# Attention of a hybrid transformer block: stacked query operands, a pinned last score group, and key tiles in reverse

## The chip, the cores and the metric

The kernel runs on one core of a Trainium2 chip. TensorE multiplies matrices (in the profile: PE, with PEld for the loading of the stationary operand), VectorE is DVE, ScalarE is ACT, GpSimd is POOL, and SyncE (SP) issues most transfers from memory. [...] The metric is the device time of one launch in microseconds: a median of repeated runs, beside one execution that was profiled.

## The reference

Two layers, each of a mixer and a gated feed-forward part, on 512 tokens of width 1024. The mixer projects the tokens and splits them over three kinds of heads: eight dilated attention heads of width 64, four retention heads and four gated linear attention (GLA) heads. The attention heads are what the change touches:

```python
qa = apply_rope(split_heads(qa, N_HEADS_A), cos_a, sin_a)
ka = apply_rope(split_heads(ka, N_HEADS_A), cos_a, sin_a)
va = split_heads(va, N_HEADS_A)
ya = merge_heads(head_norm(dilated_attention(qa, ka, va)))
...
scores = jnp.einsum('bhrnqd,bhrnkd->bhrnqk', qb, kk).astype(jnp.float32) * (d ** -0.5)
...
p = jnp.exp(scores - m[..., None])
l = p.sum(-1)
o = jnp.einsum('bhrnqk,bhrnkd->bhrnqd', p, vv) / l[..., None]
```

The three dilated branches are weighted by their denominators and summed. With 512 tokens this equals one causal softmax in which a key counts as often as branches see it; the kernel holds these counts in a constant table (`mult`).

The mixer's output goes through `w_out`, a residual and a layer norm; then a feed-forward part follows with a three-tap causal convolution and a gate, again with a residual and a norm.

## The kernel before, in words

**Precision.** The large products run with float32r operands, each value split into a high part and the rounded rest, the low part. `mm3` (lines 211 to 214) adds three products: high by high, high by low, low by high. A weight tile comes by DMA into `raw`, ScalarE casts it to `whi` (line 198), and VectorE subtracts to get `wlo` (line 199). The tokens stand in `xth` and `xtl`, transposed. In the profile's names the moving operand comes first: `acc<-xth,whi` streams tokens against stationary weights (the query and key projections of the heads), `acc<-whi,xth` streams weights against stationary tokens (v, gates, output).

**Attention, by pairs of heads.** Head pair p holds heads 2p and 2p+1, on the partition rows 0 to 63 and 64 to 127. `project_heads(g)` (lines 588 to 611) makes two pairs: for query and key it runs 8 x 3 matmuls into an `acc` bank, turns the result by the rotary tables (ScalarE copies at line 604, VectorE at 605 to 607), casts it to a high part `qk` (line 608) and subtracts for the low part (line 610).

`scores` (lines 613 to 645) goes through the query tiles of 128 tokens in three groups: tile 3, tile 2, tiles 0 and 1 together. For every tile and both heads it issues three products with 64 rows (line 629): high query by high key, high query by low key, low query by high key. Each group takes two `bank`s, one for each head, out of four; VectorE reads a bank with the mask and takes the row minimum (line 638), ScalarE takes the exponential (line 641), VectorE multiplies by the counts and sums (line 642).

`weighted` (lines 647 to 682) transposes the probabilities on TensorE (line 286), ScalarE copies them out (line 671), and products with v (line 659) are summed over the key tiles in one bank, in the groups key tile 0, key tiles 1 and 3, key tile 2. Then follow a copy, transposes back, and `finish` with the norm of the head; `finish_rows` transposes the finished rows for the output projection.

**What sets the order.** The kernel is written as a program without an order of its own between engines: a planner takes, on every engine, the instruction with the lowest priority number among those it holds to be ready by its own estimate of the times, and gives out buffers as it goes. `at(n)` sets the number from which the next instructions count. What results is a fixed list for every engine, and each engine works its list in order. `tc.issue_after(x)` forces the instructions traced in its block to stand behind instruction x on x's engine. In a layer the numbers are: heads 0 and 1 at 5000, scores of pair 0 at 6000 and pair 1 at 6400, v at 7000, heads 2 and 3 at 8000, scores of pair 2 at 9000 and pair 3 at 9400, gates at 9200, output projection at 20000.

**Buffers.** `x4` has three tiles of 128 x 4 x 512, for the query and key operands, for v, and for the norms' gains `gb` (loaded by GpSimd's queue, line 740); `bank` has four PSUM banks for scores, transposes and attention output; `page` has nine tiles of 128 x 512.

Of the kernel before, what the change touches and what calls it, by code (L numbers as in the profile page):

```python
# [17 lines left out]
P = 128  # L18
# [131 lines left out]
def hymba(ctx: ExitStack, tc: tile.TileContext, x, xt, wpk, prm, wal, lnv, cst, out):  # L150
# [59 lines left out]

    def mm3(ps, ah, al, bh, bl, first, last):
        nc.tensor.matmul(ps, ah, bh, start=first, stop=False)  # L212
        nc.tensor.matmul(ps, ah, bl, start=False, stop=False)  # L213
        nc.tensor.matmul(ps, al, bh, start=False, stop=last)  # L214
# [199 lines left out]
    for l in range(DEPTH):  # L414
# [173 lines left out]
        def project_heads(g):  # L588


            qk = x4("qk", F32R)
            low = [None] * 4
            for u in range(2):
                kt = chunk(l, f"heads{2 * g + u}")
                for qk_ in range(2):
                    b = 2 * qk_ + u
                    ps = acc()
                    ms = slice(qk_ * P, (qk_ + 1) * P)
                    for k in range(KD):
                        h_, l_ = kt[k]  # L600
                        mm3(ps, h_[:, ms], l_[:, ms], xth[:, k, :], xtl[:, k, :], k == 0, k == KD - 1)
                    turned, a = page("rope"), page("rope")
                    for r in range(4):
                        A.copy(turned[32 * r:32 * r + 32, :], ps[32 * (r ^ 1):32 * (r ^ 1) + 32, :])
                    V.tensor_mul(a, ps, C("ropea_c"))
                    V.tensor_mul(turned, turned, C("ropea_s"))
                    V.tensor_add(a, a, turned)
                    A.copy(qk[:, b, :], a)
                    low[b] = page("yrg", 512, F32R)
                    V.tensor_sub(low[b], a, qk[:, b, :].bitcast(F32))  # L610
            return qk, low

        def scores(qk, low, u, l3):


            probs = [[None] * NT, [None] * NT]
            nmx = small(8, "s_at")
            for group in ((3,), (2,), (0, 1)):
                scs = [bank(), bank()]
                prs, o = [page(), page()], 0  # L620
                for i in group:
                    n, m = (i + 1) * P, max(256, (i + 1) * P)
                    ts = slice(i * P, (i + 1) * P)
                    for step in range(3):
                        for hh in range(2):
                            hs = slice(hh * 64, hh * 64 + 64)
                            q_ = (low[u][hs, ts] if step == 2 else qk[hs, u, ts])
                            k_ = (low[2 + u][hs, 0:m] if step == 1 else qk[hs, 2 + u, 0:m])
                            mmul(scs[hh][:, o:o + m], q_, k_, start=step == 0, stop=step == 2)  # L629
                    for hh in range(2):  # L630
                        probs[hh][i] = (scs[hh][:, o:o + n], prs[hh][:, o:o + n])
                    o += m
                for hh in range(2):
                    for i in group:
# [3 lines left out]
                        V.tensor_tensor_reduce(out=p_, in0=s_, in1=C("neg")[:, m0:], op0=ALU.add, op1=ALU.min,  # L638
                                               scale=-0.125, scalar=3e38, accum_out=mx)
                        with tc.issue_after(tables.ins):  # L640
                            A.activation(out=p_, in_=p_, func=AF.Exp, scale=-1.0, bias=mx)
                        V.tensor_tensor_reduce(out=p_, in0=p_, in1=C("mult")[:, m0:], op0=ALU.mult, op1=ALU.add,
                                               scale=1.0, scalar=0.0, accum_out=l3[:, i, hh:hh + 1])
                        probs[hh][i] = p_
            return probs

        def weighted(pr, c0):


            groups = ((0,), (1, 3), (2,))  # L650
# [48 lines left out]
        for g in range(2):  # L699
            at(base + 5000 + 3000 * g)  # L700
            qk, low = project_heads(g)
            if g == 0:
                at(base + 7000)
                vv = x4("v")
                kt = chunk(l, "v")
                for t in range(NT):
                    centred(project(kt, t, 512), vv[:, t, :], "s_v")
            for u in range(2):
                at(base + 6000 + 3000 * g + 400 * u)
                p2 = 2 * g + u  # L710
# [7 lines left out]

        at(base + 9200)
        kt = chunk(l, "gates")  # L720
        for t in range(NT):
            ps = project(kt, t, 512)
            g = page("rope")
            with tc.issue_after(tables.ins):
                A.activation(out=g, in_=ps, func=AF.Tanh, scale=0.5)
            V.scalar_tensor_tensor(out=g, in0=g, scalar=1.0, in1=ps, op0=ALU.add, op1=ALU.mult)
            V.tensor_mul(ynat[t], ynat[t], g)
# [134 lines left out]
```

## Time and profile before

| | us |
|---|---|
| median of 3 runs | 1248.39 (1246.88 to 1251.35) |
| profiled execution, whole time | 1247.36 |
| its span | 1245.6 |
| PE busy | 1227.3 |
| DVE busy | 785.2 |
| ACT busy | 490.6 |
| granted TensorE clock | 0.997 of full |

The span is the time from the first to the last instruction of the profiled execution. A timeline row reads: start, duration, engine, line, operation, result and operands, shape of the stationary tile and of the moving one, count; in brackets the idle time of the engine before it and what ended that. Matmuls overlap in the pipeline, so the cost of one is the distance to the next one's start and not its duration. A row with x2 holds two instructions merged. A row of the waits reads: who waited for whom, total us, times, longest us. In the rows of groups the numbers after the bar are busy us, mean ns of one, and idle us of the engine before them.

In the first layer the span's stages on TensorE around the change are: projection of heads 0 and 1 (until 100.6 us, mixed with the retention and GLA products), scores of pair 0, v (102.1 to 131.2), heads 2 and 3 (131.2 to 166.6, with the scores of pair 1 from 135.5), scores of pair 2, gates (168.0 to 199), scores of pair 3 (from 199.4), output projection (from 204.4).

### The profile page before, as it was taken

To read this page: it belongs to the slowest core of one execution; us is meant where nothing else is said; L and a number is where in the kernel's file an instruction comes from. 1 tells how busy PE (TensorE), PEld (TensorE's weight loads), DVE (VectorE), ACT (ScalarE), POOL (GpSimd) and SP (SyncE) were. 2 spreads that over 40 slices of the span, in tenths; PEclk is the share of its full clock that TensorE was granted. 3 is DMA by queue.
4 is the path that set the end of the run, shared out by engine and by line. 5 is a ranking of instruction groups with operands and counts; after the bars stand their busy time and mean duration, and the time that the engine had idled before them with its cause. 6 is when DMAs were issued, how large, how long until landed. Compare 5 with 4: busy or idle time off the path is not lost.

```text
span 1245.6 us, 15209 instructions
## 1 busy us (share of the span) xinstructions
PE 1227.3 (99%) x5956; PEld 999.1 (80%) x5956; DVE 785.2 (63%) x1451; ACT 490.6 (39%) x689; POOL 17.0 (1%) x26
## 2 busy tenths in 40 slices
PE   9999999999999999999999999999999999999997
PEld 7877677898888888888887776778988888888885
DVE  6685776777663356664767857677766633566636
ACT  4434565145442134442153446552444421444410
POOL 0000000000000000000000000000000000000000
PEclk9999999999999999999999999999999999999998
DMA  8411313223332333232142113131333323333221
GB/s 293 131 64 34 118 51 99 72 74 130 100 89 91 93 111 91 87 100 77 62 132 88 34 43 128 34 119 51 102 117 89 100 76 98 114 102 102 93 77 68
DMA packets 33399, 116.27 MB, mean 93 GB/s; under 512 B 3728, under 2 KB 4144, under 8 KB 33200
## 3 DMA queue, kind: packets, MB, share of 16 engines
q1 hardware_dynamic: 32176, 111.11, 28.5%
q0 software_dynamic: 1152, 4.19, 0.9%
q8 instruction: 47, 0.77, 0.2%
q14 instruction: 24, 0.20, 0.1%
HBM read 113.20 MB, written 2.10 MB: 93 GB/s over the span
## 4 chain that ended last, share of the span: by engine, by line
PE 91%; DVE 4%; DMA 2%; ACT 2%; issue 0%; SPq 0%; DVEq 0%; ACTq 0%
PE acc L214 25%; PE acc L213 25%; PE acc L212 25%; PE bk L286 3%; PE side L213 2%; PE side L212 2%; PE side L214 2%; DMA raw<-in_wpk 2%; PE bk L659 2%; DVE wlo L199 1%; ACT whi L198 1%; DVE pg L638 1%; PE bk L565 1%; PE bk L545 1%; PE bk L561 1%; PE bk L629 1%
## 5 line engine op out<-in xcount | busy, mean ns | idle before, releaser
L199 DVE TENSOR_TENSOR wlo<-raw,whi 128x1024 fp32r<-128x1024 f32 (+2 forms) x201 | 240.1, 1195 | 218.7 <-ACT whi L198 217.4
L213 PE MATMUL acc<-xtl,whi 128*128 128x512 f32 (+1 forms) x896 | 341.8, 382 | 0.0
L212 PE MATMUL acc<-xth,whi 128*128 128x512 f32 (+1 forms) x896 | 341.7, 382 | 0.0
L214 PE MATMUL acc<-xth,wlo 128*128 128x512 f32 (+1 forms) x896 | 339.6, 379 | 0.0
L198 ACT CAST whi<-raw 128x1024 fp32r<-128x1024 f32 (+2 forms) x201 | 206.2, 1026 | 321.0 <-PE side L214 139.8
L214 PEld LDWEIGHTS acc<-xth,wlo 128*128 128x128 f32 x896 | 168.6, 188 | 35.2 <-issue 4.0
L213 PEld LDWEIGHTS acc<-xtl,whi 128*128 128x128 f32 x896 | 168.6, 188 | 34.2 <-issue 3.5
L212 PEld LDWEIGHTS acc<-xth,whi 128*128 128x128 f32 x896 | 168.4, 188 | 31.8 <-issue 1.5
L212 PE MATMUL acc<-whi,xth 128*128 128x512 f32 (+1 forms) x256 | 94.4, 369 | 0.6 <-ACT whi L198 0.6
L213 PE MATMUL acc<-wlo,xth 128*128 128x512 f32 (+1 forms) x256 | 94.3, 368 | 0.7 <-DVE wlo L199 0.7
L214 PE MATMUL acc<-whi,xtl 128*128 128x512 f32 (+1 forms) x256 | 94.7, 370 | 0.0
L212 PE MATMUL acc<-whi,yt 128*128 128x512 f32 x238 | 93.2, 393 | 0.0
L213 PE MATMUL acc<-wlo,yt 128*128 128x512 f32 x238 | 92.3, 389 | 0.0
L214 PE MATMUL acc<-whi,yt 128*128 128x512 f32 x238 | 92.3, 389 | 0.0
L765 DVE SCALAR_TENSOR_TENSOR pg<-acc,prm,pg 128x511 f32<-128x511 f32 x86 | 64.2, 747 | 31.7 <-ACT pg L764 31.7
L764 ACT ACTIVATE pg<-acc,prm 128x512 f32<-128x512 f32 x86 | 66.8, 777 | 26.3 <-PE acc L214 26.3
L766 DVE SCALAR_TENSOR_TENSOR pg<-acc,prm,pg 128x510 f32<-128x510 f32 x86 | 64.4, 749 | 3.0
L388 DVE SCALAR_TENSOR_TENSOR x<-x,acc 128x512 f32<-128x512 f32 x38 | 26.1, 686 | 59.7 <-PE acc L214 59.7
L213 PEld LDWEIGHTS acc<-wlo,xth 128*128 128x128 f32 x256 | 48.1, 188 | 9.2 <-DVE wlo L199 1.1
L212 PEld LDWEIGHTS acc<-whi,xth 128*128 128x128 f32 x256 | 48.3, 189 | 8.8 <-issue 1.0
L214 PEld LDWEIGHTS acc<-whi,xtl 128*128 128x128 f32 x256 | 48.1, 188 | 8.7 <-issue 1.2
L212 PE MATMUL acc<-whi,yrg 128*128 128x512 f32 x138 | 54.5, 395 | 0.0
(176 smaller groups left out, 1541.4 us busy)
## 6 DMA issues: line engine op xcount, KB each, us to landing
raw<-in_wpk SPq DMA_DIRECT2D x188, 512.0 KB, 3.6
gb<-in_lnv POOLq DMA_DIRECT2D x8, 512.0 KB, 4.7
x<-in_x SPq DMA_DIRECT2D x4, 512.0 KB, 6.3
raw<-in_wpk SPq DMA_DIRECT2D x8, 256.0 KB, 2.8
out<-x SPq DMA_DIRECT2D x8, 256.0 KB, 2.0
raw<-in_wpk SPq DMA_DIRECT2D x4, 408.0 KB, 3.3
xraw<-in_xt SPq DMA_DIRECT2D x3, 512.0 KB, 7.4
cst<-in_cst SPq DMA_DIRECT2D x1, 1478.0 KB, 9.3
```

The source lines that it names most:

```text
L198: nc.scalar.copy(hi, raw)
L199: lo_engine.tensor_sub(lo, raw, hi.bitcast(F32))
L212: nc.tensor.matmul(ps, ah, bh, start=first, stop=False)
L213: nc.tensor.matmul(ps, ah, bl, start=False, stop=False)
L214: nc.tensor.matmul(ps, al, bh, start=False, stop=last)
L286: nc.tensor.transpose(dst, src, ident)
L388: V.scalar_tensor_tensor(out=xr, in0=xr, scalar=scale, in1=ps, op0=ALU.mult, op1=ALU.add)
L545: mmul(sc, kT[:, ts], qbd, start=True, stop=True)
L659: mmul(oT[hh * 64:hh * 64 + 64, j * P:], vv[:, j, c0 + hh * 64:c0 + hh * 64 + 64], pts[hh][:, o:o + n], start=j == 0, stop=js == groups[-1])
L764: A.activation(out=u, in_=ps, func=AF.Identity, scale=w(2), bias=w(3))
L765: V.scalar_tensor_tensor(out=u[:, 1:], in0=ps[:, :S - 1], scalar=w(1), in1=u[:, 1:], op0=ALU.mult, op1=ALU.add)
L766: V.scalar_tensor_tensor(out=u[:, 2:], in0=ps[:, :S - 2], scalar=w(0), in1=u[:, 2:], op0=ALU.mult, op1=ALU.add)
```

## The change

- `project_heads` makes one pair at a time and writes four operands into one `x4` tile. For head A of the pair, `qA` holds the high query in rows 0 to 63 and the low query in rows 64 to 127, `kA` the high key in both halves. `qB` and `kB` are the same for head B with the halves exchanged. `kl` holds the low keys of both heads.
- `scores` forms a score tile from one product with 128 rows (high and low query by high key) and one with 64 rows (high query by low key). Query tiles 3 and 2 are issued as one block, all 128-row products first and then the 64-row ones; tiles 0 and 1 follow in a block of the same form.
- The block of tiles 0 and 1 is forced behind a given product on TensorE: for pair 0 behind the fourth `mm3` of v, for pair 1 behind the eleventh of heads 2 and 3, for pair 2 behind the fourth of the gates; pair 3 has none. For this the gates' code stands ahead of the scores of pairs 2 and 3 in the source; priorities are as before.
- `weighted` goes through the keys as tiles 2 and 3, then tile 1, then tile 0.

```diff
+    made = []
+
     def mm3(ps, ah, al, bh, bl, first, last):
         nc.tensor.matmul(ps, ah, bh, start=first, stop=False)
         nc.tensor.matmul(ps, ah, bl, start=False, stop=False)
-        nc.tensor.matmul(ps, al, bh, start=False, stop=last)
+        made.append(nc.tensor.matmul(ps, al, bh, start=False, stop=last).ins)
...
-        def project_heads(g):
-            qk = x4("qk", F32R)
-            low = [None] * 4
-            for u in range(2):
-                kt = chunk(l, f"heads{2 * g + u}")
...
-                    A.copy(qk[:, b, :], a)
-                    low[b] = page("yrg", 512, F32R)
-                    V.tensor_sub(low[b], a, qk[:, b, :].bitcast(F32))
-            return qk, low
+        def project_heads(p):
+            four = x4("qk", F32R)
+            qA, qB, kA, kB = (four[:, i, :] for i in range(4))
+            kl = page("yrg", 512, F32R)
+            up, dn = slice(0, 64), slice(64, 128)
+            kt = chunk(l, f"heads{p}")
...
+                if b == 0:
+                    A.copy(qA[up], a[up])
+                    A.copy(qB[dn], a[dn])
+                    V.tensor_sub(qA[dn], a[up], qA[up].bitcast(F32))
+                    V.tensor_sub(qB[up], a[dn], qB[dn].bitcast(F32))
+                else:
+                    A.copy(kA[up], a[up])
+                    A.copy(kB[dn], a[dn])
+                    A.copy(kA[dn], a[up])
+                    A.copy(kB[up], a[dn])
+                    V.tensor_sub(kl[up], a[up], kA[up].bitcast(F32))
+                    V.tensor_sub(kl[dn], a[dn], kB[dn].bitcast(F32))
+            return qA, qB, kA, kB, kl
 
-        def scores(qk, low, u, l3):
+        def scores(parts, l3, behind):
+            qA, qB, kA, kB, kl = parts
...
-            for group in ((3,), (2,), (0, 1)):
...
-                    for step in range(3):
-                        for hh in range(2):
-                            hs = slice(hh * 64, hh * 64 + 64)
-                            q_ = (low[u][hs, ts] if step == 2 else qk[hs, u, ts])
-                            k_ = (low[2 + u][hs, 0:m] if step == 1 else qk[hs, 2 + u, 0:m])
-                            mmul(scs[hh][:, o:o + m], q_, k_, start=step == 0, stop=step == 2)
+            def products(banks, places, half):
+                for i, (g_, o) in places.items():
+                    m = max(256, (i + 1) * P)
+                    ts = slice(i * P, (i + 1) * P)
+                    for hh in range(2):
+                        hs = slice(hh * 64, hh * 64 + 64) if half else slice(0, P)
+                        mmul(banks[g_][hh][:, o:o + m], (qA, qB)[hh][hs, ts], (kl, kl)[hh][hs, :m] if half else (kA, kB)[hh][:, :m],
+                             start=not half and o == 0, stop=half and i > 0)
+
+            for groups in (((3,), (2,)), ((0, 1),)):
...
+                with tc.issue_after(behind) if behind and len(groups) == 1 else nullcontext():
+                    for half in (False, True):
+                        products(banks, places, half)
...
-            groups = ((0,), (1, 3), (2,))
+            groups = ((2, 3), (1,), (0,))
...
-                             pts[hh][:, o:o + n], start=j == 0, stop=js == groups[-1])
+                             pts[hh][:, o:o + n], start=j == 2, stop=j == 0, skip_group_check=True)
...
-        for g in range(2):
-            at(base + 5000 + 3000 * g)
-            qk, low = project_heads(g)
-            if g == 0:
+        marks = {}
+        for two in range(2):
+            if two == 0:
+                at(base + 5000)
+                parts = [project_heads(p) for p in range(2)]
                 at(base + 7000)
                 vv = x4("v")
+                marks["v"] = len(made)
...
+                at(base + 8000)
+                marks["heads"] = len(made)
+                parts += [project_heads(p) for p in range(2, 4)]
+            else:
+                at(base + 9200)
+                marks["gates"] = len(made)
+                kt = chunk(l, "gates")
...
-                pr = scores(qk, low, u, l3)
+                name, n = (("v", 3), ("heads", 10), ("gates", 3), (None, 0))[p2]
+                pr = scores(parts[p2], l3, made[marks[name] + n] if name else None)
                 finish_rows()
                 o = weighted(pr, p2 * P)
                 finish(o, ll, p2)
```

More of the change, by code (lines that the diff above doesn't have):

```diff
@@ L1 @@
 import math
-from contextlib import ExitStack
+from contextlib import ExitStack, nullcontext
 import numpy as np
@@ L585, in hymba @@
                 nc.sync.dma_start(out=xres[t], in_=x[t * P:(t + 1) * P, :])
-        def project_heads(g):
-            qk = x4("qk", F32R)
-            low = [None] * 4
-            for u in range(2):
-                kt = chunk(l, f"heads{2 * g + u}")
[L595 to L608, printed above, removed]
-                    low[b] = page("yrg", 512, F32R)
-                    V.tensor_sub(low[b], a, qk[:, b, :].bitcast(F32))
-            return qk, low
@@ L613, in scores @@
-        def scores(qk, low, u, l3):
+        def project_heads(p):
[4 more added lines that the diff above has]
+            kt = chunk(l, f"heads{p}")
+            for b in range(2):
+                ps = acc()
+                ms = slice(b * P, (b + 1) * P)
+                for k in range(KD):
+                    h_, l_ = kt[k]
+                    mm3(ps, h_[:, ms], l_[:, ms], xth[:, k, :], xtl[:, k, :], k == 0, k == KD - 1)
+                turned, a = page("rope"), page("rope")
+                for r in range(4):
+                    A.copy(turned[32 * r:32 * r + 32, :], ps[32 * (r ^ 1):32 * (r ^ 1) + 32, :])
+                V.tensor_mul(a, ps, C("ropea_c"))
+                V.tensor_mul(turned, turned, C("ropea_s"))
+                V.tensor_add(a, a, turned)
+                if b == 0:
[11 more added lines that the diff above has]
+            return qA, qB, kA, kB, kl
@@ L707, in hymba @@
                     centred(project(kt, t, 512), vv[:, t, :], "s_v")
+                at(base + 8000)
[5 more added lines that the diff above has]
+                kt = chunk(l, "gates")
+                for t in range(NT):
+                    ps = project(kt, t, 512)
+                    g = page("rope")
+                    with tc.issue_after(tables.ins):
+                        A.activation(out=g, in_=ps, func=AF.Tanh, scale=0.5)
+                    V.scalar_tensor_tensor(out=g, in0=g, scalar=1.0, in1=ps, op0=ALU.add, op1=ALU.mult)
+                    V.tensor_mul(ynat[t], ynat[t], g)
             for u in range(2):
-                at(base + 6000 + 3000 * g + 400 * u)
-                p2 = 2 * g + u
+                at(base + 6000 + 3000 * two + 400 * u)
+                p2 = 2 * two + u
                 ll = small(8, "s_at")
                 l3 = ll.rearrange("p (i h) -> p i h", h=2)
-                pr = scores(qk, low, u, l3)
+                name, n = (("v", 3), ("heads", 10), ("gates", 3), (None, 0))[p2]
+                pr = scores(parts[p2], l3, made[marks[name] + n] if name else None)
                 finish_rows()
@@ L719, in hymba @@
         at(base + 9200)
[L720 to L727, printed above, removed]
         for k in range(4):
```

18 lines of the change are left out of this document (10 added, 8 removed).

## The prediction

> **What bounds the kernel now.** I read the page first: which engine fills the span, and what the chain that ended last is made of.
>
> ```profile
> span 1245.6 us, 15209 instructions
> PE 1227.3 (99%) x5956; PEld 999.1 (80%) x5956; DVE 785.2 (63%) x1451; ACT 490.6 (39%) x689; POOL 17.0 (1%) x26
> PE 91%; DVE 4%; DMA 2%; ACT 2%; issue 0%; SPq 0%; DVEq 0%; ACTq 0%
> ```
>
> TensorE is busy for 1227.3 of 1245.6 us and holds 91% of the chain. So time is won only where TensorE's instructions become fewer or cheaper, or where it stands still. Next I asked who TensorE waits for, over the whole span.
>
> ```profile
> PE bk L629 <- DVE s_at L638: 4.4, 6, 0.9
> ```
>
> The largest wait is in attention: score products (L629) standing behind the VectorE pass that reads an earlier score bank (L638), three times in each layer. Being "busy" also hides slow stretches, since the ends of matmuls are modelled, so the third view is TensorE's timeline, where I read the distance from one start to the next. Here is head pair 0 of the first layer, with the VectorE row it waits for.
>
> ```profile
> 100.12 0.39 PE L213 MATMUL acc<-xtl,whi 128*128 128x512 f32 x1
> 100.35 0.39 PE L214 MATMUL acc<-xth,wlo 128*128 128x512 f32 x1
> 100.67 0.50 PE L629 MATMUL bk<-qk 64*128 64x512 f32 x2
> 101.00 0.40 PE L629 MATMUL bk<-yrg,qk 64*128 64x512 f32 x2
> 101.24 0.40 PE L629 MATMUL bk<-qk,yrg 64*128 64x512 f32 x2
> 101.47 0.34 PE L629 MATMUL bk<-qk 64*128 64x384 f32 x2
> 101.63 1.23 DVE L199 TENSOR_TENSOR wlo<-raw,whi 128x1024 fp32r<-128x1024 f32 x1
> 101.65 0.34 PE L629 MATMUL bk<-yrg,qk 64*128 64x384 f32 x2
> 101.83 0.34 PE L629 MATMUL bk<-qk,yrg 64*128 64x384 f32 x2
> 102.10 0.50 PE L212 MATMUL acc<-whi,xth 128*128 128x512 f32 x1
> 102.43 0.40 PE L213 MATMUL acc<-wlo,xth 128*128 128x512 f32 x1
> 102.77 0.68 DVE L638 CUSTOM_DVE_ANT_0 pg<-bk,cst 128x512 f32<-128x512 f32 x1
> 103.52 0.38 PE L629 MATMUL bk<-qk 64*128 64x256 f32 x1 [0.69 <-DVE s_at L638]
> ...
> 104.59 0.28 PE L629 MATMUL bk<-qk 64*128 64x256 f32 x1
> 104.71 0.28 PE L629 MATMUL bk<-yrg,qk 64*128 64x256 f32 x1
> ...
> 105.04 0.50 PE L214 MATMUL acc<-whi,xtl 128*128 128x512 f32 x1
> 105.38 0.40 PE L212 MATMUL acc<-whi,xth 128*128 128x512 f32 x1
> ```
>
> Three things are to be seen. **Slots:** a pair of 64-row products, one for each head, takes one slot ("x2"): 512 columns 0.23 us (101.24 to 101.47), 384 columns 0.18, 256 columns 0.12. **Switches:** going from 128-row to 64-row products costs about 0.2: 100.35 to 100.67 is 0.32 where a projection takes 0.23 (100.12 to 100.35), and the first slot takes 0.33 where the next takes 0.24. Coming back costs the same (101.83 to 102.10 is 0.27 for 0.18, then 102.10 to 102.43 is 0.33 for 0.23). **The last group** (query tiles 0 and 1) finds its banks full, because VectorE was converting weights until 102.86; TensorE, which works in order, stands still. The second head's bank comes free later still, so its products do not pair with the first head's: 103.52 to 105.04 is 1.52 for twelve products that as six pairs would take 6 x 0.12 = 0.72.
>
> **The change part by part.**
>
> *Stacking on 128 rows.* Before, a head's score tile is three 64-row products, six for a pair of heads, in three slots. After, it is one 128-row product for each head (two slots, nothing to pair with) and one 64-row product for each head (one slot, if paired): three slots again. For query tiles 3 and 2 that is 3 x 0.23 + 3 x 0.18 = 1.23 both before and after. A 128-row product is taken to cost what a 64-row slot of the same width does, as the projection's 0.23 shows for 512. So 24 products become 16 and save nothing by themselves.
>
> *Last group behind a given product.* Pair 0's goes behind the fourth product triple of v, pair 1's behind the eleventh triple of heads 2, pair 2's behind the fourth of the gates. Twelve products after 102.10 are 12 x 0.23 = 2.76, so pair 0's last group starts near 104.9. Its banks are emptied by two passes of 0.68 that began at 102.77, at about 104.1. Both are then free: no wait, and the heads pair. What it defers is work behind DVE and ACT that nothing on TensorE stands waiting for.
>
> So a pair of heads after costs 1.23 + 0.72 + four switches (into and out of 64 rows, twice) of 0.2 = 2.75. The 128-row half follows the projections without a switch, having their tile (128*128). Before, pair 0 cost 105.38 - 100.35 = 5.03, less the four projection products in it (4 x 0.23 = 0.92): 4.11. **Saved 1.36.**
>
> Pairs 2 and 1 are read in the same way:
>
> ```profile
> 166.27 0.39 PE L214 MATMUL acc<-xth,wlo 128*128 128x512 f32 x1
> 166.59 0.50 PE L629 MATMUL bk<-qk 64*128 64x512 f32 x2
> ...
> 169.67 0.38 PE L629 MATMUL bk<-qk 64*128 64x256 f32 x1 [0.92 <-DVE s_at L638]
> ...
> 171.18 0.50 PE L214 MATMUL acc<-whi,xtl 128*128 128x512 f32 x1
> 171.52 0.40 PE L212 MATMUL acc<-whi,xth 128*128 128x512 f32 x1
> ```
> ```profile
> 135.49 0.50 PE L629 MATMUL bk<-qk 64*128 64x512 f32 x2
> ...
> 139.38 0.44 PE L629 MATMUL bk<-qk 64*128 64x384 f32 x1 [0.62 <-DVE s_at L638]
> ...
> 142.00 0.40 PE L212 MATMUL acc<-xth,whi 128*128 128x512 f32 x1
> ```
>
> Pair 2: 171.52 - 166.27 = 5.25, less 0.92 is 4.33; saved 4.33 - 2.75 = **1.58**. Pair 1: 142.00 - 135.49 = 6.51 with nine projection products (2.07) in between is 4.44. But its wait is on the second head of query tile 2, whose bank pair 0's output still holds; the change does not move that group behind anything. If the wait (0.62) and its two extra switches (0.4) stay, the pair costs 3.77 and saves 0.67; if they go, 1.69. I take 0.7, the row that stays.
>
> Pair 3 gets no product to stand behind, and the gates end just before it:
>
> ```profile
> 200.50 0.69 DVE L727 TENSOR_TENSOR yt<-yt,rope 128x512 f32<-128x512 f32 x1
> 201.25 0.33 PE L286 MATMUL side<-cst,yt 128*128 128x128 f32 x1 [0.57 <-DVE yt L727]
> 202.74 0.75 DVE L349 SCALAR_TENSOR_TENSOR yrg<-side,prm,yrg 128x512 fp32r<-128x512 f32 x1 [0.33 <-ACT yrg L348]
> 204.44 0.50 PE L212 MATMUL acc<-whi,yrg 128*128 128x512 f32 x1
> ```
>
> The output projection cannot start before the row that L349 ends at 203.49; it starts at 204.44. Cheaper scores there only leave TensorE idle until 203.49: between 0 and 0.95 saved, I take 0.4.
>
> *Operand preparation.* For each pair of heads ScalarE makes six half-height casts instead of two full ones, VectorE four half-height subtractions instead of two:
>
> ```profile
> L604 ACT COPY rope<-acc 32x512 f32<-32x512 f32 x64 | 37.0, 577 | 13.9 <-PE acc L214 13.0
> L608 ACT CAST qk<-rope 128x512 fp32r<-128x512 f32 x16 | 10.0, 625 | 18.3 <-DVE rope L607 18.3
> L610 DVE TENSOR_TENSOR yrg<-rope,qk 128x512 fp32r<-128x512 f32 x16 | 11.0, 686 | 1.4 <-ACT qk L608 1.4
> 165.00:175.00 10.00, 9.08 (x53) 6.95 (x52) 9.97 (x22) 6.73 (x12) 0.00 (x0) 1.00 0.36 107
> 161.09 0.62 ACT L608 CAST qk<-rope 128x512 fp32r<-128x512 f32 x1 [2.09 <-DVE rope L607]
> ```
>
> A 32-row copy (0.577) takes nearly what a 128-row one does (0.625), so rows do not pay: per pair of heads ACT gets 4 x 0.6 = 2.4 us more and DVE 2 x 0.69 = 1.4. The cover is the projections that lie between a pair's preparation and its scores: pair 1's scores start at 135.49, 33 us after v's first product (102.10), which follows both preparations on TensorE. Pair 2 is tight: its key cast starts at 161.09, its scores at 166.59, and in 165 to 175 (the row's third engine) VectorE is busy 9.97 of 10 us. Four casts and a subtraction end at 161.09 + 2.4 + 0.7 = 164.2 if nothing cuts in, and some 3 us later if heads 3's four copies (2.3 us) go first. The cost is between 0 and 2.5 us a layer; I take 0.5, since the planner can put gate products ahead.
>
> *Keys from the last tile to the first.* Key tiles 2 and 3 need only the probabilities of query tiles 2 and 3, which are ready first; key tile 0 needs all. The transposes, the products and their columns stay the same in number. What it could give back are small slips before transposes, 0 to 0.3 a layer; I take 0.
>
> *Buffers.* Four stacked operand tiles a layer share three x4 slots with v: heads 2 waits for pair 0's scores, heads 3 for pair 1's, tens of us before either writes. The norm's gains (gb) now wait for pair 2's scores instead of pair 1's:
>
> ```profile
> POOL gb L740 <- PE bk L629: 248.3, 4, 62.6
> L363 DVE SCALAR_TENSOR_TENSOR x<-x,s_ln,gb x32: 739/744/745, 241.5 to 1239.0; 128x512 f32<-128x512 f32 x32
> ```
>
> They are first read at 241.5, so a load issued after pair 2's scores (171.18) costs nothing; on POOL only the other half of gb stands behind it. The weights' loads on SP's queue keep their order, since the stages keep their priorities.
>
> **Sum.** A layer saves 1.36 + 0.7 + 1.58 + 0.4 - 0.5 = 3.5, two layers 7.1. The profiled execution took 1247.36 us in all, its span plus 1.8; so about 1240.3. The median of the runs, 1248.39, lies 1.0 above that execution, which is within their spread; I predict 1240.
>
> **The rivals.**
>
> *More is won (about 1235).* Pair 1's wait and switches go too (+1.0), pair 3 gives its whole 0.95 (+0.55), preparation stays hidden (+0.5), the slips before transposes go (+0.3): 2.35 more a layer, 4.7 in all, 1240.3 - 4.7 = 1235.6. For it: with tiles 3 and 2 issued as one block, everything after is later and finds banks free. Against: pair 1's bank is held by something that the change does not touch.
>
> *The products do not stay in blocks (about 1247, no change).* The order on TensorE is the planner's. If a bank comes free late, it can issue half-height products between full ones: each group then enters and leaves 64 rows twice, four more switches for a pair of heads, 4 x 0.2 x 8 pairs = 6.4, and 1240.3 + 6.4 = 1246.7. Before, pair 1 was split in this way. [...]
>
> *Slower (about 1252).* Pair 2's operands come late, and TensorE stands before its first score product, because the order was fixed for an earlier arrival. VectorE, full from 165 to 175, has 4 x 1.4 = 5.5 us more to do in each layer; if that all queues ahead of pair 2's key subtraction and behind weight conversions, TensorE loses up to 6 a layer, 1240.3 + 12 = 1252. The point from which it decides is an idle of 3.5 + 0.5 = 4.0 us a layer there. Against: gate weights are needed by TensorE at the same time and can be put ahead; half of the 5.5 belongs to pairs whose preparation is long over.
>
> **How the numbers follow.** Forecast 0.52, more 0.22, no change 0.15, slower 0.11. About 0.3%, 3.7 us, is what a measurement of this kernel can tell from no change: faster means below 1244.6. The forecast's own range is 1237 to 1244, nearly all below that line; with the first rival faster has 0.73, same 0.16, slower 0.11. The range for 8 in 10 runs from 1231, a little under the first rival, since the unknown costs of order lie on both sides, to 1249, above the no-change case and short of the slower one.
>
> **What would show it.** Right: no wait of a score product on L638 before the last group of pairs 0 and 2; there 128-row pitches of 0.12 and "x2" half-height products; 16 score products for each pair of heads; attention from the first score to the output projection's first product shorter by 3 to 4 us in each layer. Wrong: a new wait of TensorE on the casts or subtractions of q and k; more than four switches in a pair; VectorE's conversions (L199) waited for by projections; or pair 3's region taking up what the others gave.

## The result, and the profile after

The changed kernel takes 1241.42 us (median; 1239.9 to 1243.3), beside 1247.72 us for the kernel before: a ratio of 0.9939, interval 0.9921 to 0.9956. A second measurement (changed_again, below) gave 1241.07 us and 0.9929 (0.9912 to 0.9945). It is faster, by 0.6 to 0.7%. The profiled execution of the changed kernel was its slowest, 1243.3 us with a span of 1241.5; why is told with the stages.

The page of the changed kernel, the line of busy times:

```profile
PE 1224.1 (99%) x5892; PEld 996.8 (80%) x5892; DVE 794.6 (64%) x1467; ACT 509.8 (41%) x721; POOL 17.1 (1%) x26
```

TensorE still bounds the kernel, with 64 instructions fewer; ScalarE and VectorE got 19 and 9 us more to do. Here is who TensorE waits for in the changed kernel:

```profile
PE bk L288 <- DVE s_at L660: 2.3, 4, 0.7
PE bk L288 <- DVE s_at L664: 1.6, 2, 0.8
PE bk L639 <- DVE s_at L660: 1.2, 2, 0.6
```

L639 are the score products, L660 the mask pass that empties a score bank, L664 the multiplication by the counts, L288 the transposes. The wait of score products on the mask pass went from 4.4 us to 1.2, and the two that are left are pair 3's, one in each layer. But the transposes of the probabilities now wait for 3.9 us, and before they hardly waited, as two groups of the list of lines show (busy us, mean ns, then the idle time before them and who ended it). First the kernel before, transposes and products with v, then the changed kernel:

```profile
L286 PE MATMUL bk<-cst,pg 128*128 128x128 f32 x240 | 35.2, 276 | 0.2
L659 PE MATMUL bk<-pg,v 128*64 128x512 f32 (+3 forms) x128 | 24.4, 448 | 0.0
```
```profile
L288 PE MATMUL bk<-cst,pg 128*128 128x128 f32 x240 | 36.9, 279 | 4.0 <-DVE s_at L660 2.3 <-DVE s_at L664 1.6
L681 PE MATMUL bk<-pg,v 128*64 128x256 f32 (+3 forms) x128 | 22.0, 448 | 0.0
```

**The wait was partly handed on.** And the same 128 products with v, of the same shapes, are busy for 2.4 us less, though neither the stacking nor the pins touch them. One of them lasts as long as before (448 ns); more of them overlap.

How pair 0 of the first layer looks now, on TensorE's timeline of the changed kernel (the answer to the prediction's third fence):

```profile
100.75 0.96 PE L639 MATMUL bk<-qk 128*128 128x512 f32 x4
101.64 0.68 PE L639 MATMUL bk<-yrg,qk 64*128 64x512 f32 x4
102.25 0.50 PE L214 MATMUL acc<-whi,xth 128*128 128x512 f32 x1
102.59 0.40 PE L215 MATMUL acc<-wlo,xth 128*128 128x512 f32 x1
...
105.14 0.63 PE L639 MATMUL bk<-qk 128*128 128x256 f32 x4
...
106.14 0.50 PE L214 MATMUL acc<-whi,xth 128*128 128x512 f32 x1
```

The products stand in two blocks, the second directly behind the twelfth product of v, without a wait. The blocks take 1.50 (100.75 to 102.25) and 1.00 us (105.14 to 106.14), and the first projection product behind each takes 0.1 longer than its usual 0.23 (102.25 to 102.59): 2.7 in all.

Next, the stages of layer 1, cut at the first projection product of v, of heads 2, of the gates, of the output projection and of what follows it; the gates are cut once more where their products end. The columns are the stretch, its length, then busy us of PE, PEld, DVE, ACT and POOL with instructions, the granted clock, DMA share and GB/s. Before:

```profile
102.10:131.20 29.10, 28.41 (x139) 21.98 (x137) 16.32 (x46) 11.61 (x21) 0.00 (x0) 1.00 0.13 38
131.20:168.02 36.82, 36.08 (x190) 25.84 (x188) 27.67 (x74) 24.41 (x41) 1.25 (x2) 1.00 0.34 112
168.02:198.95 30.93, 30.01 (x155) 23.20 (x153) 19.84 (x57) 15.06 (x27) 0.00 (x0) 1.00 0.14 38
198.95:204.44 5.49, 4.69 (x33) 3.39 (x31) 4.30 (x10) 3.97 (x6) 0.00 (x0) 1.00 0.49 175
204.44:257.68 53.24, 53.24 (x266) 42.86 (x265) 40.25 (x102) 18.18 (x30) 1.05 (x2) 1.00 0.26 81
```

After:

```profile
102.25:129.38 27.13, 26.33 (x131) 20.95 (x129) 17.84 (x48) 13.72 (x25) 0.00 (x0) 1.00 0.18 58
129.38:164.96 35.58, 35.55 (x181) 25.71 (x179) 26.45 (x73) 26.01 (x43) 0.00 (x0) 1.00 0.24 74
164.96:196.44 31.48, 30.32 (x154) 22.78 (x152) 23.14 (x62) 18.46 (x33) 1.25 (x2) 1.00 0.24 71
196.44:200.69 4.25, 3.62 (x18) 2.18 (x16) 3.33 (x9) 3.11 (x5) 0.00 (x0) 0.99 0.66 218
200.69:255.87 55.18, 55.18 (x269) 44.54 (x269) 41.39 (x103) 19.21 (x31) 1.05 (x2) 0.97 0.26 78
200.70:204.20 3.50, 3.50 (x12) 2.87 (x12) 2.19 (x7) 1.92 (x3) 1.05 (x2) 0.52 0.51 110
```

The stages of v and of heads 2 and 3 give 1.97 + 1.24 = 3.21 us. The gates with pair 3 give only 0.69 (36.42 to 35.73), and the output projection takes 1.94 more. The last row says where: for its first 3.5 us the granted clock averages 0.52. If it is at one half for x us and full for the rest, (3.5 - x/2) / 3.5 = 0.52 gives x = 3.4, so 1.7 us are lost. Layer 2 loses the same, from 815 us on (a granted clock of 0.51 from 815.0 to 818.5 us). In a second profile of the same kernel (changed_again) the output projection runs at full clock:

```profile
201.30:254.94 53.64, 53.64 (x269) 43.27 (x269) 41.53 (x105) 19.44 (x31) 1.05 (x2) 1.00 0.26 81
```

The 0.40 that it still takes more than before are four transposes of the gated rows (those of the retention and GLA heads, `side<-cst,yt`), which stood ahead of the output projection and now stand inside it. So a layer gives 3.21 + 0.69 - 0.40 = 3.5 us at full clock, and 3.21 + 0.69 - 1.94 = 1.96 with the half clock; twice that is 3.9 of the 4.1 us between the two profiled spans.

### The profile page after: what moved, and what is told of

Read it like the earlier page. It is cut to its first block, busy times and chain, and to the rows that moved or that the text cites. A ratio compares the mean times of both kernels' runs of the same rounds, so it can differ in the third digit from the quotient of the medians.

```text
span 1241.5 us, 15145 instructions
## 1 busy us (share of the span) xinstructions
PE 1224.1 (99%) x5892; PEld 996.8 (80%) x5892; DVE 794.6 (64%) x1467; ACT 509.8 (41%) x721; POOL 17.1 (1%) x26
## 4 chain that ended last, share of the span: by engine, by line
PE 94%; DVE 3%; ACT 1%; DMA 1%; issue 1%; SPq 0%; DVEq 0%; ACTq 0%
PE acc L214 26%; PE acc L215 26%; PE acc L216 26%; PE bk L288 3%; PE side L214 2%; PE side L216 2%; PE side L215 2%; PE bk L681 2%; PE bk L639 1%; DMA raw<-in_wpk 1%; PE bk L567 1%; PE bk L547 1%; PE bk L563 1%; DVE wlo L199 1%; PE bk L553 1%
## 5 line engine op out<-in xcount | busy, mean ns | idle before, releaser
L214 PE MATMUL acc<-xth,whi 128*128 128x512 f32 (+1 forms) x896 | 340.8, 381 | 0.0
L216 PE MATMUL acc<-xth,wlo 128*128 128x512 f32 (+1 forms) x896 | 340.1, 380 | 0.0
L216 PEld LDWEIGHTS acc<-xth,wlo 128*128 128x128 f32 x896 | 168.6, 188 | 35.8 <-issue 5.5
L214 PEld LDWEIGHTS acc<-xth,whi 128*128 128x128 f32 x896 | 168.3, 188 | 32.7 <-issue 2.0
L214 PE MATMUL acc<-whi,xth 128*128 128x512 f32 (+1 forms) x256 | 95.0, 371 | 0.8 <-ACT whi L198 0.8
L216 PE MATMUL acc<-whi,xtl 128*128 128x512 f32 (+1 forms) x256 | 94.1, 368 | 0.0
L214 PE MATMUL acc<-whi,yt 128*128 128x512 f32 x238 | 93.2, 393 | 0.0
L216 PE MATMUL acc<-whi,yt 128*128 128x512 f32 x238 | 92.4, 389 | 0.0
L214 PEld LDWEIGHTS acc<-whi,xth 128*128 128x128 f32 x256 | 48.1, 188 | 9.6 <-issue 1.2
L214 PE MATMUL acc<-whi,yrg 128*128 128x512 f32 x138 | 55.5, 402 | 0.0
L215 PE MATMUL acc<-wlo,yrg 128*128 128x512 f32 x138 | 54.9, 397 | 0.0
```

The source lines that it names most:

```text
L216: made.append(nc.tensor.matmul(ps, al, bh, start=False, stop=last).ins)
```

## The experiments

**One part of the change at a time.** *stack_only* keeps only the stacking, without pins and with the old order of keys; *no_pin* keeps stacking and the reversal; *keys_old* stacking and the pins.

```diff
# no_pin
-                pr = scores(parts[p2], l3, made[marks[name] + n] if name else None)
+                pr = scores(parts[p2], l3, None)
# keys_old
-            groups = ((2, 3), (1,), (0,))
+            groups = ((0,), (1, 3), (2,))
# stack_only: both
```

> Stacked operands alone: no pin, key groups as before. If the pin wins and stacking only spares the unpaired half, 1245 to 1247, 1 to 3 us under the kernel before. If stacking wins by itself, about 1242. If its casts and subtractions come late for pair 2, over 1248, with score products waiting on them.

> The changed kernel with no group pinned behind a product. Theory A, that the pin is what wins: score products wait again on the mask pass of an earlier bank, three times a layer, 4.4 us in all as in the kernel before, and the time is about 1246. Theory B, that the stacked operands win, since a 128-row product needs no partner: an unpaired last group costs 0.24 us instead of 0.8 more, and the time is about 1242 to 1243.

> The changed kernel with the key groups as before (0; 1 and 3; 2). Theory A, that the reversal is of no account: within 1 us of the changed kernel's 1241.4. Theory B, that the reversal puts transposes ahead of probabilities that are not ready: the waits of transposes (line 288) on VectorE, 3.9 us over the span in the changed kernel's profile, go, and the time is 1238 to 1239. Theory C, that the reversal is what makes the pinned last group cheap: 1244 or more.

Measured: stack_only 1248.92 us, ratio 1.0 (0.9988 to 1.0012); no_pin 1244.37 us, 0.9959 (0.9944 to 0.9974); keys_old 1243.47 us, 0.9952 (0.9935 to 0.9969). The waits of TensorE in stack_only, then in no_pin, then in keys_old:

```profile
PE bk L639 <- DVE s_at L660: 4.6, 8, 0.9
```
```profile
PE bk L639 <- DVE s_at L660: 3.0, 6, 0.6
```
```profile
PE bk L288 <- DVE s_at L664: 3.0, 4, 0.8
PE bk L639 <- DVE s_at L660: 1.7, 4, 0.6
```

What follows: in the measured time stacking by itself is worth nothing, and the score products go on waiting as before (4.6 us). But the profile of stack_only, with a span of 1248.5 us and a mean clock of 0.993, has three stretches at half clock: behind pair 3 in both layers (an estimate from the mean durations of products that follow, which the last section gives), and in layer 2 also behind pair 2's scores, as this row shows:

```profile
787.60:791.10 3.50, 3.50 (x12) 2.69 (x12) 3.47 (x9) 2.48 (x5) 1.12 (x2) 0.53 0.27 96
```

Each costs about 1.7 us, by the working above. Without them the span would be about 1243.4 us (an estimate); the kernel before, whose profile has none in the attention (clock 1.00 from 100 to 225 us and from 715 to 845), spans 1245.6. So stacking may save some 2 us at full clock, which the half clock takes back here; its 12 executions have mean clocks of 0.992 to 0.997, those of the kernel before beside them 0.994 to 0.998.

In the times either of the other two parts alone brings 0.4 to 0.5%, and both together 0.6 to 0.7% (the intervals of one and of both overlap). At full clock they about add up: from the first score product of layer 1 to the first product of its output projection TensorE takes 103.77 us before, 102.72 in stack_only (0.40 of the difference are the four transposes that moved), 101.60 in no_pin, 101.18 in keys_old and 99.94 in the changed kernel. Against stack_only that is 1.12 for the reversal, 1.54 for the pins and 2.78 for both.

With the pins the wait moves from the score products to the transposes, in either order of the keys: 3.9 us in the changed kernel, 3.8 in keys_old, and only 0.5 in no_pin. So the reversal does not cause it (theory B of keys_old). With the old order key tile 0 comes first and needs the probabilities of the group that was just deferred, as keys_old's timeline shows for pair 0:

```profile
112.58 0.33 PE L288 MATMUL bk<-cst,pg 128*128 128x128 f32 x1 [0.68 <-DVE s_at L664]
```

And the group of products with v stands in keys_old as in the kernel before, while in no_pin it stands as in the changed kernel. keys_old, then no_pin:

```profile
L681 PE MATMUL bk<-pg,v 128*64 128x512 f32 (+3 forms) x128 | 24.4, 447 | 0.0
```
```profile
L681 PE MATMUL bk<-pg,v 128*64 128x256 f32 (+3 forms) x128 | 22.0, 448 | 0.0
```

So these 2.4 us belong to the reversal. Before, key tile 0 is a block by itself: its four products take 1.32 us, where four steps of 0.23 are 0.92. The timeline of the kernel before:

```profile
113.84 1.38 PE L659 MATMUL bk<-pg,v 128*64 128x512 f32 x4
115.16 0.66 PE L286 MATMUL bk<-cst,pg 128*128 128x128 f32 x4
```

Reversed, tiles 1 and 0 come last, when all probabilities are there, and are issued as one block; in layer 1 the products with v stand in eight blocks instead of ten.

**Without stacking, pins and reversal kept.** *unstacked* has the old three 64-row products and the old two casts and two subtractions, in the changed kernel's order.

```diff
-                    for half in (False, True):
-                        products(banks, places, half)
+                    for step in range(3):
+                        products(banks, places, step)
```

> The changed kernel with its pins, its two blocks and its reversed keys, but with three 64-row products for each head and score tile in place of one of 128 and one of 64 rows, and operands prepared as before (two full casts, two full subtractions for a pair of heads). Theory A: three slots either way, so stacking saves nothing once the pins let the heads pair, and ScalarE and VectorE have less to do: within 1 us of the changed kernel (ratio to before 0.993 to 0.995). Theory B: the 128-row products, which need no partner, carry part of the gain: 2 us slower than the changed kernel (ratio 0.996).

Measured: 1244.39 us, 0.9962 (0.995 to 0.9974), some 3 us more than the changed kernel, as theory B has it. But the score products themselves aren't what costs. The largest loss is in the stage of heads 2 and 3, around pair 1: 35.58 us in the changed kernel. The rows of unstacked, the stage and the rows around its waits:

```profile
129.46:166.60 37.14, 36.15 (x193) 25.87 (x191) 26.76 (x73) 24.45 (x40) 0.00 (x0) 1.00 0.22 72
```
```profile
137.80 0.44 PE L628 MATMUL bk<-qk 64*128 64x384 f32 x1 [0.33 <-DVE s_at L649]
...
142.85 0.50 PE L628 MATMUL bk<-qk 64*128 64x256 f32 x4
...
143.76 0.98 PE L288 MATMUL bk<-cst,pg 128*128 128x128 f32 x7
...
145.81 0.52 PE L288 MATMUL bk<-cst,pg 128*128 128x128 f32 x3 [0.60 <-DVE s_at L649]
```

The last group of three 64-row slots takes 0.91 us (142.85 to 143.76), against 0.99 when stacked (141.94 to 142.93). By the distances between starts all score products of this stage take 4.48 us here and 4.64 in the changed kernel. What is lost, 1.56 in this stage, holds two waits of 0.93 together, and the planner's order around pair 1 differs. That made two theories: stacking is worthless and the order is to blame, or 64-row products have a price between other products that the slots don't show. The last two runs return to this.

**The half clock behind pair 3.** Two ways to fill the stretch between gates and output projection. *out_rows* lets the output projection begin with the rows of head pairs 0 and 1, which are long finished, ahead of the four gated rows, so that it can start while pair 3's scores wait; *fill* puts ten products there whose result nobody reads (work added, nothing left out); *before_out_rows* makes the row order of out_rows in the kernel before.

```diff
# out_rows, before_out_rows
-        w[f"out{h}"] = [(ks, c) for ks in (PAIRS[2], PAIRS[3], PAIRS[0], PAIRS[1])]
+        w[f"out{h}"] = [(ks, c) for ks in (PAIRS[0], PAIRS[2], PAIRS[3], PAIRS[1])]
-        order = (4, 5, 6, 7, 0, 1, 2, 3)
+        order = (0, 1, 4, 5, 6, 7, 2, 3)
# fill
+        at(base + 9500)
+        spare = acc()
+        with tc.issue_after(made[marks["gates"] + 31]):
+            for _ in range(10):
+                mmul(spare, xth[:, 0, :P], xth[:, 1, :], start=True, stop=True)
```

> The changed kernel, its output projection beginning with the rows of head pairs 0 and 1, which are ready, ahead of the four gated rows (the row tiles go 0, 1, 4, 5, 6, 7, 2, 3 and the weights' tiles with them). Theory A: the stretch after the gates is a hole on TensorE (about 1.5 us idle) and the hole is what halves the granted clock for 3.4 us after it (1.7 us lost); filled with products both go: 3 us a layer, 1235 to 1236, granted clock 0.998, no stretch at half clock in the attention's end. Theory B: the clock is halved by something else (the 64-row products): the hole goes, the half-clock stretch stays, 1238. Theory C: the projection waits later for the gated rows all the same: 1241.

> The changed kernel with ten spare products of 128x512 in each layer, whose result nobody reads, put where TensorE has nothing to do between the gates and the output projection. Theory A, that the hole halves the clock: no stretch at half clock in the attention's end, granted clock 0.998 in every run, and the time falls, though work is added, to the undisturbed 1239.5 to 1240.5 plus at most 1 us for the spare products. Theory B, that the 64-row products or something else halve it: clocks of 0.995 to 0.997 stay and the time is 1242 or more.

> The kernel before, with only the row order of the output projection changed (0, 1, 4, 5, 6, 7, 2, 3). Theory: it has the same hole after its gates, 5.5 us long with some 3 us of useful work, so filling it saves 1.5 to 2.5 us a layer and the half-clock stretches that its slower runs show: 1243 to 1245, little spread, clock 0.998. Rival: its score products, unpaired, fill the hole and nothing is won: 1248.

> The changed kernel itself on the chip of these runs, for the spread: the fastest executions (clock 0.998) near 1240, others in steps of about 1.7 us above, as halved stretches of the clock come or stay away; ratio to before 0.993 to 0.995.

Measured: out_rows 1238.35 us, 0.9912 (0.9897 to 0.9927); fill 1242.94 us, 0.9953 (0.994 to 0.9965); before_out_rows 1249.14 us, 1.0003 (0.9992 to 1.0014); the changed kernel once more 1241.07 us. First the changed kernel's timeline at this place:

```profile
198.62 0.51 PE L639 MATMUL bk<-qk 128*128 128x256 f32 x2 [0.61 <-DVE s_at L660]
...
201.28 0.63 PE L215 MATMUL acc<-wlo,yrg 128*128 128x512 f32 x1
201.71 0.63 PE L214 MATMUL acc<-whi,yrg 128*128 128x512 f32 x1
```

and in the second profile of the same kernel, changed_again:

```profile
201.64 0.40 PE L215 MATMUL acc<-wlo,yrg 128*128 128x512 f32 x1
201.87 0.39 PE L214 MATMUL acc<-whi,yrg 128*128 128x512 f32 x1
```

The same instructions in the same order stand 0.43 us apart in one execution and 0.23 in the other. The clock, then, doesn't follow from the kernel alone. In out_rows the hole is filled with work that has to be done anyway:

```profile
198.09 0.68 PE L639 MATMUL bk<-yrg,qk 64*128 64x512 f32 x4
198.69 0.50 PE L214 MATMUL acc<-whi,yt 128*128 128x512 f32 x1
```

Products of the output projection (`whi,yt`) stand directly behind pair 3's first block, before its last group; no wait is left there, the pitch of these products is 0.23 to 0.24 (199.04 to 199.28 to 199.51) behind the first's 0.35, and the mean clock of its five executions is 0.997 to 0.998. The time is the one that theory B gave; theory B's sign, a half-clock stretch that stays, is not to be seen in these rows. The spare products of fill took the score products' wait away too, and its six executions have mean clocks of 0.997 to 0.998, those of changed_again 0.996 to 0.998; but they cost at least what they won: 0.9953 is no better than the changed kernel's 0.9939. In before_out_rows the order on TensorE hardly moved: the planner kept all score products of pair 3 ahead of the output projection (in its timeline the last of them starts at 203.57 us and the projection at 203.88), so nothing was won: the gain of out_rows needs an order in which other products really come between.

**The waits that moved to the transposes.** *tuned* is out_rows with the first transposes of pairs 0 and 2 put behind a later product of v and of the gates, and the transposes of pair 1's finished rows behind another product of the gates; *pins_only* is the same with the old row order of the output projection.

```diff
+                    with tc.issue_after(late) if late and js == groups[0] else nullcontext():
...
-                finish_rows()
-                o = weighted(pr, p2 * P)
+                with tc.issue_after(made[marks["gates"] + 7]) if p2 == 2 else nullcontext():
+                    finish_rows()
+                t_ = (("v", 14), (None, 0), ("gates", 14), (None, 0))[p2]
+                o = weighted(pr, p2 * P, made[marks[t_[0]] + t_[1]] if t_[0] else None)
```

> The kernel with the output rows 0, 1 first, and in addition the first transposes of pair 0 and pair 2 (key tiles 2 and 3) pinned behind the fifteenth product triple of v and of the gates, and the transposes of pair 1's finished rows behind the eighth of the gates: behind enough products that VectorE has done what they wait for. Theory: the three waits of 0.8, 0.65 and 0.5 us in each layer go, 4 us in all: 1234 to 1235. Rival: what the transposes feed is then late itself and TensorE waits there: 1238.

> The fastest kernel so far with the output rows in the old order (4, 5, 6, 7, 0, 1, 2, 3): the pins of the transposes alone. Theory: the pins are worth 2 us a layer and the filled hole 1.2 us undisturbed, more where the clock halves after the hole: 1237 to 1239, with clocks from 0.998 down to 0.995 and so a wider spread than the 0.1 us of the filled kernel. Rival: pins and hole depend on each other and it is at 1241.

Measured: tuned 1234.15 us (1234.12 to 1234.2), 0.988 (0.9866 to 0.9894); pins_only 1237.11 us, 0.9898 (0.9881 to 0.9915). tuned beats both kernels of this case. In its waits only this is left of attention:

```profile
PE bk L288 <- DVE yt L351: 1.1, 2, 0.6
```

So the waits before transposes and before pair 3's scores were real losses: taking them away, by work put in front and not by fewer instructions, brought 1241.07 down to 1234.15, some 4 us of it by the pins (pins_only) and 3 by the filled hole.

**Stacking once more.** *tuned_unstacked* is tuned with 64-row thirds and pair 1's transposes also put behind a product; *tuned_unstacked2* also pins pair 1's first block and the first transpose of the gated rows. Two of the edits from the first to the second:

```diff
-                name, n = (("v", 3), ("heads", 10), ("gates", 3), (None, 0))[p2]
+                name, n = (("v", 3), ("heads", 13), ("gates", 3), (None, 0))[p2]
...
-                t_ = (("v", 14), ("heads", 15), ("gates", 14), (None, 0))[p2]
+                t_ = (("v", 14), ("heads", 18), ("gates", 14), (None, 0))[p2]
```

> The fastest kernel so far (output rows 0, 1 first, first transposes of pairs 0 and 2 and the finished rows pinned) with three 64-row products for each head and score tile instead of the stacked operands; its first transposes of pair 1 are pinned too, behind the sixteenth product triple of heads 2 and 3, since without stacking they waited there. Theory A: score products take the same slots, and what the kernel without stacking lost (2 to 3 us) were waits of transposes that the planner happened to place early; pinned, stacking is worth under 1 us: 1234 to 1235.5 (ratio to before 0.988 to 0.9895). Theory B: stacking itself saves TensorE time: 1237 or more.

> The scores are three 64-row products again, and the placements that cost the earlier version without stacking its time are mended: pair 1's twelve-slot first block stands whole behind the products before the last third, its last group and its transposes behind given products of that stretch, the first side transpose behind a later gates product. If stacking itself is worth nothing beside the slots of the scores (theory A), only those placements made the 64-row version slower, and this one comes to 1235 to 1236.5 us, within 2 us of the stacked version's 1234.2; the heads stage is back at about 35.5 us from 36.8. If the 64-row products carry a price of their own between the other products (theory B), the stage stays above 36.3 us and the time at 1238 us or more.

Measured: 1239.25 us, 0.9918 (0.9901 to 0.9935), and 1239.27 us, 0.9918 (0.9903 to 0.9934). By the time alone this speaks for a price of the 64-row products. The stages say where. First those of v and of heads 2 and 3 in tuned, whose span is 1232.4 us:

```profile
101.78:127.84 26.06, 26.06 (x130) 21.16 (x129) 17.85 (x48) 13.81 (x25) 0.00 (x0) 1.00 0.19 60
127.84:163.34 35.50, 35.50 (x181) 25.72 (x180) 26.50 (x73) 26.04 (x43) 0.00 (x0) 1.00 0.24 75
```

then in tuned_unstacked2, span 1237.7 us, and the rows of its timeline around pair 1:

```profile
102.14:128.18 26.04, 26.04 (x134) 21.03 (x133) 16.33 (x46) 11.51 (x21) 0.00 (x0) 1.00 0.18 60
128.18:165.96 37.78, 36.91 (x193) 25.90 (x191) 28.19 (x74) 24.94 (x41) 0.00 (x0) 1.00 0.22 70
```
```profile
150.05 1.25 PE L671 MATMUL bk<-pg,v 128*64 128x256 f32 x8 [0.43 <-ACT pg L684]
...
152.25 1.60 PE L671 MATMUL bk<-pg,v 128*64 128x384 f32 x4
154.45 1.08 PE L671 MATMUL bk<-pg,v 128*64 128x512 f32 x4
```

In the stage of v, which holds pair 0's last group, its transposes and its first products with v in the same blocks, the two agree within 0.02 us: three 64-row slots and the stacked products cost the same. In the stage with pair 1 the 64-row version loses 2.28 us in this layer alone, of 5.3 between the spans of both layers. There products with v wait for a copy of ScalarE (0.43), and the last two key tiles fall apart into two blocks again. By the distances between starts the score products of this stage take 4.73 us, a wait of 0.34 among them, against 4.60 in tuned; the products with v take 1.06 more, the transposes 0.64, and the projection products next to the blocks 0.44. So the slots are not where the time goes. The time itself, though, came out as the theory of a price has it, and whether some order gives the 64-row version the stacked one's time was not settled in two attempts: it stays open.

## Why the prediction was right, and where it was not

The time, 1241.42 beside a predicted 1240, came out, and so did the 3.5 us a layer at full clock; but the terms behind it hold errors that cancel, and that the sum came out so near is in part luck. The sign "shorter by 3 to 4 us in each layer" is there: 103.77 to 99.94 in layer 1. Pairs 0 and 1 were put at 2.06 a layer, and their stages gave 3.21; pair 2, pair 3 and the preparation were put at 1.58 + 0.4 - 0.5 = 1.48, and the rest gave 0.29 (0.69 - 0.40).

**Slots, switches and the pin of pair 0: right for its scores.** 2.7 us were predicted as 2.75. But pair 0's first transposes now wait 0.80 for the probabilities in each layer (the 1.6 us of L664). "Save nothing by themselves" holds for the slots and for the ratio of stack_only, 1.0; at full clock its profile leaves room for some 2 us, and no run shows where these come from.

**Pair 1: right in kind, and won a little more.** It stays split, but without its wait: both waits of L639 that are left are pair 3's. Read as the prediction did, it costs about 3.4 us instead of 4.44, so it saves about 1.0 where 0.7 was taken.

**Keys reversed: put at nothing, and worth about 1.1 us a layer** (no_pin beside stack_only). "Stay the same in number ... I take 0" overlooked that fewer and fuller blocks of the same products cost less: 24.4 to 22.0 us of busy time, 0.3 for each pair of heads. This is most of what v and heads gave beyond 2.06: by the distances between starts their products with v take 6.14 us before and 5.11 after.

**Pair 2: the step that failed.** The sentence that what the pin defers is work "that nothing on TensorE stands waiting for" is where it broke. Its scores no longer wait, but the transposes behind them do, in the changed kernel's timeline; the first row are those of pair 1's finished rows, the second those of pair 2's key tiles 2 and 3:

```profile
169.43 0.66 PE L288 MATMUL bk<-cst,pg 128*128 128x128 f32 x4 [0.51 <-DVE s_at L660]
...
174.85 0.55 PE L288 MATMUL bk<-cst,pg 128*128 128x128 f32 x3 [0.65 <-DVE s_at L660]
```

0.51 + 0.65 = 1.16 of the predicted 1.58 goes back, and the stage of the gates is no shorter (30.93 before, 31.48 after, with three transposes of the gated rows that moved into it). VectorE, which the prediction itself had at 9.97 of 10 us busy here, is what is late: it was read for the operands' preparation and not for the mask passes that empty the banks. tuned shows the remedy: other work in front of the transposes.

**Pair 3: the size about right, the half clock not foreseen.** The stretch from the end of the gates to the output projection became shorter by 1.24 us (5.49 to 4.25). But seven of the eight transposes of gated rows that stood in it have left it: three into the gates (0.42 at its start before, 198.95 to 199.37) and four into the output projection (0.40). What is left is about 0.4, as taken (an estimate from these rows). Where the half clock follows, 1.7 is lost, which the prediction has nowhere. Between executions this comes and goes: the changed kernel's spans go from 1237.6 us at a mean clock of 0.998 to 1241.5 at 0.995.

**Preparation: no score product waits for it, but its cost is open.** A half-height cast takes 0.62 us and a half-height subtraction 0.69, so the sizes were right. But on VectorE two such subtractions for pair 3's key stand directly ahead of the mask pass that the second wait above ends on:

```profile
173.51 0.69 DVE L622 TENSOR_TENSOR yrg<-rope,qk 64x512 fp32r<-64x512 f32 x1
174.23 0.56 DVE L660 CUSTOM_DVE_ANT_0 pg<-bk,cst 128x384 f32<-128x384 f32 x1
```

The waits don't need them, since in unstacked, with the old preparation, transposes wait too (2.9 us for the mask pass, 1.4 for the probabilities). What part of them the added subtractions cause was not measured.

**The rivals.** "More is won" named slips before transposes as something to go; in fact they grew. "Not in blocks" holds only for pairs 1 and 3. "Slower" needed a wait of pair 2's scores on their casts, which isn't there.

## What to carry to other kernels

A wait in a fixed order doesn't vanish when its instruction is moved back: look at what the late result feeds next and move that too; here stacking with pins on the scores gave 0.5%, with the order of keys 0.6 to 0.7%, with pins on the transposes and a filled hole 1.2%. Count how many blocks a group of small products falls into, not only the products: here 128 products were busy for 22.0 us instead of 24.4 when, in layer 1, ten blocks became eight. A hole in a TensorE-bound kernel may cost more than its idle time, so give it work that has to be done anyway: here TensorE was idle for 0.63 of 4.25 us, and where the half clock followed, some 1.7 us more were lost. And a ratio of 1.0 can hide a gain: look at the clock of the profiled execution (0.993 in stack_only) before a part of a change is called worthless.

## What the hardware showed that was not expected

The granted clock fell to one half behind the hole (0.52 from 200.70 to 204.20 us) without TensorE ever standing still for long: the longest wait was 0.61 us, and in the 4.25 us ahead TensorE was busy for 3.62. The half clock lasted about 3.4 us and cost 1.7, by the working with the stages. Of the two profiles of the changed kernel, with the same hole, one has it in both layers, at a mean clock of 0.995; the other has a clock of 1.00 in layer 1's output projection and 0.998 in the mean.

Mean durations show it as well. The last product of each `mm3` whose row stands in `yrg`, as the first rows of the changed kernel's output projection do (L216, in the kernel before L214; 138 in all), lasts 400 ns in the mean in the changed kernel and 398 in stack_only, 394 to 395 in no_pin, keys_old and unstacked, which have the hole too, and 392 in the kernel before. In out_rows and tuned, where other products fill the hole, it lasts 390; there the projection begins with a row in `yt`, and the L216 products on `yt` last 389 to 390, beside 389 in the changed kernel. So stack_only should have the half clock behind pair 3 in both layers, no_pin, keys_old and unstacked in one each, and out_rows and tuned in none (an estimate from these means).

It is not tied to this hole alone: stack_only has it also behind pair 2's scores (0.53 from 787.60 to 791.10 us); the longest wait of its score products is 0.9 us. Nor does a wait of this length always bring it: in the changed kernel the 0.80 us of pair 0's transposes are not followed by it (clock 1.00 from 110 to 116 us). In the last 6.6 us of the profile before and the last 6.5 after, where TensorE runs no product, the clock is 0.50 too. The cause is not shown further than this.
